# A hybrid decoder layer: turning the first two chunks by a matmul with a diagonal of the norm's powers

## The chip, the core and the metric

The kernel runs on one core of a Trainium2 chip. Such a core has a matrix engine (TensorE, PE in the profile), which multiplies a stationary 128x128 block by a moving one and writes to the accumulator memory PSUM; VectorE (DVE), ScalarE (ACT) and GpSimd (POOL) for element-wise work; and SyncE (SP), which here issues loads and stores. Each engine works through its own list of instructions in order, and waits on semaphores for the others. The metric is the device time of one execution in microseconds. The kernel before took 927.2 us, the median of three runs (926.85 to 927.48).

## The reference

One decoder layer in float32 on 512 tokens of 1024 features. Three stages follow each other, each with a norm ahead and behind it:

```python
def rms_norm(x, g):
    y = x * rsqrt(mean(x * x, axis=-1, keepdims=True) + EPS)
    return y * g

def swiglu_ffn(x, w_in, w_out):                    # w_in 1024 x 5632, w_out 2816 x 1024
    gate, up = split(x @ w_in, 2, axis=-1)
    return (silu(gate) * up) @ w_out

x = x + 0.5 * rms_norm(swiglu_ffn(rms_norm(x, norm_pre[0]), ffn1_w_in, ffn1_w_out), norm_post[0])
x = x + rms_norm(token_mixer(rms_norm(x, norm_pre[1]), ...), norm_post[1])
x = x + 0.5 * rms_norm(swiglu_ffn(rms_norm(x, norm_pre[2]), ffn2_w_in, ffn2_w_out), norm_post[2])
```

The change touches only the first `rms_norm` and the first products behind it. There, a token's row of x is multiplied by one number, its *power* r = (mean of squares + EPS) to the -1/2, and by the *weights* g, one per feature. The products need the result turned: features on the partitions, tokens along the free dimension.

## The kernel before

**Chunks, halves, parts.** The 512 tokens are four chunks of 128; chunk i lies in `xs[:, i, :]`, tokens on the partitions. The 1024 features are two halves of 512. Precision is kept by splitting each operand into a high part (a copy rounded to fp32r) and a low part (the rest); a product then is three matmuls, high by high, high by low and low by high. A high part is a copy, made on ACT; a low part is a subtraction on DVE. For a weight tile (128 x 4 x 256) `split` does both: `cast` has the copy (L244) and the subtraction (L245). For the turned x, `part` does them: L321 and L323, and later a plain copy for sums of halves (L325).

**The first feed-forward stage** multiplies with fewer products than the plain scheme would need, by sums and differences of quarters of weights and of x (the Strassen kind). The first column pair of the weights is done without that: four products named c1, c3, c2, c4 (in this order) for chunks 0 and 1, and e1 to e4 for chunks 2 and 3; p1 to p7 are those of the later column pairs. Each is a call of `prod` (L615), 24 matmuls of 256 columns (L628). c1 and c3 multiply the *first* half of the turned x with two weight tiles (`sq_84`, `sq_85`); c2 and c4 multiply the *second* half. c1 takes its parts in the order high by high, low weights, low x, the others in the order high by high, low x, low weights.

**The start** is written out by hand (`start`, inside a block in which the framework doesn't reorder), so the order of the code is the order on each engine. Ahead of it, `gain_pe` loads the row of 1024 weights and spreads it to all partitions by two matmuls with a column of ones (L123), which DVE copies from PSUM to `gpre` (L124). Then `norm(0)` and `norm(1)` run `pre`: ACT squares each half with a sum (L387); POOL makes the mean in two steps (L388) and raises it to -1/2 (L392); DVE multiplies each half by power and weights in one instruction (L403), into the tile `xn` for chunk 0 and into rows of the big buffer `hf` for chunk 1. PE turns a half by four transposes with the identity (L301, in `turn`). `spin` adds matmuls of the identity by itself (L130), whose result nobody reads; they fill PE's time at three places.

```python
self.spin(3)
step(q[0][0], q[0][1], q[0][0])   # turn chunk 0, both halves; high part of its first half
self.spin(2)
split = self.split()
step(q[1][0], q[1][1])            # turn chunk 1, both halves
next(split)                       # high part of the first weights, on ACT
step(q[1][0])                     # high part of chunk 1's first half
next(split)
step(q[0][0], q[1][0])            # low parts of both
```

After that `start` goes on: product c1, the next weights, high and low parts of the second halves, product c3, `norm(2)`, c2, `norm(3)`, and so on; chunks 2 and 3 are turned by transposes between the products (`sums`, L334 and L335). In the names of the order below, a trailing number is that of a buffer or of its use: `ps` are PSUM banks, `xn` and `hf` rows to be turned, `xq` the turned x with its parts, `sq` and `w` weights with their parts, `raw` weights as loaded, `col` single columns.

Of the kernel before, what the change touches and what calls it, by code (L numbers as in the profile page):

```python
# [11 lines left out]
ALU = mybir.AluOpType  # L12
# [12 lines left out]
EARLY = 2  # L25
HALF = T // 2
KH = ND // 2
FILL = (15, 12, 2, 2)
NH = 4
W = 512  # L30
# [41 lines left out]
class Layer:  # L72
# [37 lines left out]
    def gain_pe(self, tag, row):  # L110

        nc = self.nc
        g = self.cp.tile([P, D], F32, tag=tag, bufs=1, name=self.name(tag))
        r = self.hf[0:1, 14:16, :].rearrange("p a t -> p (a t)")
        nc.sync.dma_start(r, row)
        one = self.st("one", P)[:1]
        nc.gpsimd.memset(one, 1.0)
        self.spare = self.ps()
        self.spin(2)
        for h in range(2):  # L120
            ps = self.ps()
            v = slice(512 * h, 512 * h + 512)
            nc.tensor.matmul(ps, one, r[:, v], start=True, stop=True)  # L123
            nc.vector.tensor_copy(g[:, v], ps)  # L124
        return g

    def spin(self, n):
# [67 lines left out]
    def load(self, ld):  # L195
        self.nc.sync.dma_start(self.raw[ld.key], ld.src)

    def split(self):

        nc = self.nc  # L200
        it = self.items.popleft()
        raw = self.raw[it.key]
        _, a, b = raw.shape
        if it.dst:
            w = it.dst()
        else:
            if self.wt is None:
                self.wt = self.wp.tile([P, (2 * D + 128) * WBUF], F32R, name="w")

            n = self.free.popleft()  # L210
            o = PAD + (2 * D + 128) * n - 16 * (it.late if it.late is not None else b == 512)
            w = self.wt[:, o : o + 2 * D].rearrange("p (b k t) -> p b k t", b=2, k=a)
            if it.apart:
                w = tuple(self.wt[:, v : v + D].rearrange("p (k t) -> p k t", k=a) for v in (o, o + D + 16))
            self.slot[id(w)] = n, w
        hi, lo = self.both(w)
        self.ready.append((w, it.dst is not None))
        rows = it.rows
        if rows is None:
            yield from self.cast(hi, lo, raw, it.defer)  # L220
# [12 lines left out]
        if it.then:  # L233
            it.then(raw)
        self.load_due(self.done)
        self.done += 1
        yield

    def cast(self, hi, lo, src, defer=False):

        nc = self.nc
        late, self.pend = self.pend, ()
        steps = [
            lambda: nc.scalar.copy(hi, src),  # L244
            lambda: nc.vector.tensor_tensor(lo, src, hi.bitcast(F32), op=ALU.subtract),  # L245
        ]
# [46 lines left out]
        nc.gpsimd.tensor_tensor(r, m, self.nhalf[:, :n], op=ALU.pow)  # L293
        return r

    def turn(self, src, h):

        pt = self.ps()
        for c in range(4):
            k = 4 * h + c  # L300
            self.nc.tensor.transpose(pt[:, c * P : (c + 1) * P], src[:, k * P : (k + 1) * P], self.ident)  # L301
        return pt.rearrange("p (c t) -> p c t", c=4)

    def two(self, dst, i, src):
# [7 lines left out]
        for h in halves:  # L312
            self.two(self.xq[2 * (i // 2) + h], i, self.turn(src, h))

    def part(self, i, h, src):

        pv = self.turn(src, h)
# [3 lines left out]
        self.nc.scalar.copy(hi, pv)  # L321
        yield
        self.nc.vector.tensor_tensor(lo, pv, hi.bitcast(F32), op=ALU.subtract)  # L323
        yield
        self.nc.scalar.copy(self.xf[h][:, :, v], pv)  # L325
        yield
# [390 lines left out]
        self.hold = ()  # L717
        self.holes()

    def start(self, norm, xn):  # L720

        norm(0)
        norm(1)
        q = [[self.part(i, h, xn[i]) for h in range(2)] for i in range(2)]
        step = lambda *gs: [next(g) for g in gs]
        self.spin(3)
        step(q[0][0], q[0][1], q[0][0])
        self.spin(2)
# [987 lines left out]
def layer(tc, aps):  # L1716
    with ExitStack() as ctx:
# [26 lines left out]
        with ExitStack() as f1:  # L1744
            L.open_ffn(f1)
            with tc.manual_schedule():
# [13 lines left out]
                L.start(norm, xn)  # L1760
# [39 lines left out]
```

## Time and profile before

| what | value |
|---|---|
| median of three runs | 927.2 us |
| the profiled execution | 926.35 us |
| its span | 924.6 us |
| PE busy | 916.0 us, 7032 instructions |
| DVE, ACT, POOL busy | 765.2, 479.9, 285.2 us |
| first product (L628) starts | 11.63 us |
| granted clock, mean | 0.998 |

The span is what the profiler recorded from the first to the last instruction; the time of an execution has 1.75 us around it. In rows of instructions stand the start, the time that they were busy, engine, line, operation, what is written and read, sizes and a count, and in brackets the idle time of the engine ahead of them with what ended it. PEld is the loading of PE's stationary blocks, which runs beside its matmuls. A matmul's record lasts longer than the step to the next one, because matmuls overlap; steps are counted from start to start.

### The profile page before, as it was taken

To read this page: it belongs to the slowest core of one execution; us is meant where nothing else is said; L and a number is where in the kernel's file an instruction comes from. 1 tells how busy PE (TensorE), PEld (TensorE's weight loads), DVE (VectorE), ACT (ScalarE), POOL (GpSimd) and SP (SyncE) were. 2 spreads that over 40 slices of the span, in tenths; PEclk is the share of its full clock that TensorE was granted. 3 is DMA by queue.
4 is the path that set the end of the run, shared out by engine and by line. 5 is a ranking of instruction groups with operands and counts; after the bars stand their busy time and mean duration, and the time that the engine had idled before them with its cause. 6 is when DMAs were issued, how large, how long until landed. Compare 5 with 4: busy or idle time off the path is not lost.

```text
span 924.6 us, 16960 instructions
## 1 busy us (share of the span) xinstructions
PE 916.0 (99%) x7032; PEld 843.1 (91%) x7032; DVE 765.2 (83%) x899; ACT 479.9 (52%) x653; POOL 285.2 (31%) x225
## 2 busy tenths in 40 slices
PE   9999999999999999999999999999999999999997
PEld 7999999999888889888888888999999999988885
DVE  6898999999869786788766655888999999976874
ACT  7644445445544455987654254853444445544441
POOL 3535565562000026000020301445455665100001
PEclk9999999999999999999999999999999999999999
DMA  9243324332322413422423135213334332232302
GB/s 320 91 138 115 115 92 136 117 115 69 100 106 90 116 46 94 113 70 71 138 71 113 47 107 190 91 45 116 115 99 130 123 106 93 69 117 100 103 23 92
DMA packets 81991, 97.10 MB, mean 105 GB/s; under 512 B 4177, under 2 KB 61557, under 8 KB 81914
## 3 DMA queue, kind: packets, MB, share of 16 engines
q1 hardware_dynamic: 81306, 94.44, 32.1%
q8 instruction: 55, 0.90, 0.4%
q0 software_dynamic: 320, 1.06, 0.3%
q10 hardware_dynamic: 288, 0.52, 0.2%
q14 instruction: 22, 0.18, 0.1%
HBM read 93.90 MB, written 2.11 MB: 104 GB/s over the span
## 4 chain that ended last, share of the span: by engine, by line
PE 98%; issue 0%; ACT 0%; DMA 0%; DVE 0%; POOL 0%; DVEq 0%; POOLq 0%; ACTq 0%
PE ps L628 46%; PE ps L134 11%; PE ps L136 11%; PE ps L135 11%; PE ps L854 6%; PE ps L464 6%; PE ps L301 1%; PE ps L477 1%; PE ps L1302 1%; PE ps L1569 0%; PE ps L123 0%; PE ps L1537 0%; PE ps L1373 0%; PE ps L1341 0%; PE ps L1539 0%
## 5 line engine op out<-in xcount | busy, mean ns | idle before, releaser
L245 DVE TENSOR_TENSOR w<-raw,w 128x1024 fp32r<-128x1024 f32 x224 | 374.4, 1682 | 52.9 <-ACT w L244 52.7
L244 ACT CAST w<-raw 128x1024 fp32r<-128x1024 f32 x224 | 233.1, 1052 | 258.5 <-POOL raw L232 104.8
L232 POOL TENSOR_TENSOR raw<-raw,raw 128x1024 f32<-128x1024 f32 x80 | 221.0, 2764 | 174.2 <-DVE w L245 163.7
L628 PE MATMUL ps<-xq,w 128*128 128x256 f32 x2016 | 238.1, 277 | 0.0
L628 PEld LDWEIGHTS ps<-xq,w 128*128 128x128 f32 x2016 | 233.7, 188 | 0.2
L628 PE MATMUL ps<-sq,w 128*128 128x256 f32 x1440 | 169.8, 276 | 0.0
L628 PEld LDWEIGHTS ps<-sq,w 128*128 128x128 f32 x1440 | 166.2, 188 | 0.0
L134 PE MATMUL ps<-w,hs 128*128 128x512 f32 x240 | 93.6, 390 | 0.0
L135 PE MATMUL ps<-w,hs 128*128 128x512 f32 x240 | 93.5, 389 | 0.0
L136 PE MATMUL ps<-w,hs 128*128 128x512 f32 x240 | 93.4, 389 | 0.0
L134 PE MATMUL ps<-w,xq 128*128 128x512 f32 x208 | 83.2, 400 | 0.1
L135 PE MATMUL ps<-w,xq 128*128 128x512 f32 x208 | 81.0, 390 | 0.0
L136 PE MATMUL ps<-w,xq 128*128 128x512 f32 x208 | 80.9, 391 | 0.0
L388 POOL TENSOR_SCALAR col<-col 128x1 f32<-128x1 f32 x24 | 6.5, 273 | 200.2 <-ACT junk L387 200.1
L136 PEld LDWEIGHTS ps<-w,hs 128*128 128x128 f32 x240 | 45.1, 188 | 9.4
L134 PEld LDWEIGHTS ps<-w,hs 128*128 128x128 f32 x240 | 45.1, 188 | 8.8
L135 PEld LDWEIGHTS ps<-w,hs 128*128 128x128 f32 x240 | 45.1, 188 | 8.7
L464 PE MATMUL ps<-xq,w 128*128 128x512 f32 (+1 forms) x240 | 49.8, 368 | 0.0
L464 PEld LDWEIGHTS ps<-xq,w 128*128 128x128 f32 x240 | 41.3, 188 | 7.6 <-issue 0.2
L136 PEld LDWEIGHTS ps<-w,xq 128*128 128x128 f32 x208 | 39.0, 188 | 8.8 <-DVE xq L308 0.3
L134 PEld LDWEIGHTS ps<-w,xq 128*128 128x128 f32 x208 | 39.1, 188 | 8.6 <-ACT xq L307 0.7
L135 PEld LDWEIGHTS ps<-w,xq 128*128 128x128 f32 x208 | 39.1, 188 | 7.3
(259 smaller groups left out, 1108.8 us busy)
## 6 DMA issues: line engine op xcount, KB each, us to landing
raw<-in_ffn_w_in_dram SPq DMA_DIRECT2D x88, 512.0 KB, 4.5
raw<-in_ffn_w_out_dram SPq DMA_DIRECT2D x44, 512.0 KB, 3.6
raw<-in_w_mix_in_dram SPq DMA_DIRECT2D x28, 512.0 KB, 3.8
raw<-in_w_mix_out_dram SPq DMA_DIRECT2D x8, 512.0 KB, 3.6
out_dram<-xs SPq DMA_DIRECT2D x8, 256.0 KB, 2.1
xs<-in_x_dram SPq DMA_DIRECT2D x6, 256.0 KB, 6.2
gpost<-in_norm_post_dram SPq DMA_DIRECT2D x3, 512.0 KB
gpre<-in_norm_pre_dram SPq DMA_DIRECT2D x2, 512.0 KB, 4.1
```

The lines of the kernel that those rows point to most:

```text
L134: mm(ps, sh, mh, start=start, stop=False, **kw)
L135: mm(ps, sh, ml, start=False, stop=False, **kw)
L136: mm(ps, sl, mh, start=False, stop=stop, **kw)
L232: nc.gpsimd.tensor_tensor(o, o, c, op=ALU.add)
L244: lambda: nc.scalar.copy(hi, src),
L245: lambda: nc.vector.tensor_tensor(lo, src, hi.bitcast(F32), op=ALU.subtract),
L301: self.nc.tensor.transpose(pt[:, c * P : (c + 1) * P], src[:, k * P : (k + 1) * P], self.ident)
L464: mm(self.cols(ps, u0, u1), self.both(w)[a][:, k, :], self.xop(k, b, u0, u1), start=k + n + m == 0, stop=k == ND - 1 and n == 2, skip_grou ...
L477: self.nc.tensor.matmul(ps[:, :HALF], self.both(w)[a][:, k, :], self.xop(k, b, 0, HALF), start=m + k == 0, stop=m == 2 and k == ND - 1)
L628: self.nc.tensor.matmul(ps[:, c], wb[b][:, k, v], left[d][:, k, :], start=first and a + n + k == 0, stop=n == 2 and k == KH - 1, skip_grou ...
L854: self.nc.tensor.matmul(out, a[:, x, ka, tok(qa, t)], b[y][:, kb, col(qb)], start=p in sums and p not in begun, stop=stop and last[p, t] = ...
L1302: nc.tensor.matmul(sc[r, o : o + u.stop - u.start], k8[:, m, r], q8[:, m, u], start=True, stop=True, skip_group_check=True)
```

## The change

- `gain_pe` only does the two matmuls. The first half of the weights is copied from PSUM by DVE, in `start`, the second by ACT (L758 of the new file).
- For chunks 0 and 1, `start` does the norm itself. ACT squares all four halves; DVE makes the means (`mean`, L735); POOL still raises to -1/2 (L738). DVE multiplies rows by the weights alone (`gain`, L741), which waits for no power, and builds a 128x128 diagonal of the chunk's powers from the identity (`diag`, L745).
- `turn` has an argument `by`. With it, each of the four blocks is turned by an ordinary f32 matmul whose moving operand is the diagonal (L304), so that turning and multiplying by the powers are one step. Chunks 2 and 3, and all later uses, keep the transposes (L302).
- Only the first halves are turned ahead of c1. The row products of the second halves come behind the weights of c1 on DVE, and their turns behind c1 on PE.
- The high part of the first weights (`sq_84`) is made by DVE instead of ACT.
- Fillers are 2, 2 and 1 instead of 2, 3 and 2.

PE, from the fillers behind the weights' row to the third product, before: turns (L301), fillers (L130), products (L628).

```order
L130 MATMUL ps_101<-ident 128x128 x3
L301 MATMUL ps_160<-ident,xn_140 128x128 x4
L301 MATMUL ps_165<-ident,xn_140 128x128 x4
L130 MATMUL ps_101<-ident 128x128 x2
L301 MATMUL ps_173<-ident,hf_82 128x128 x4
L301 MATMUL ps_178<-ident,hf_82 128x128 x4
L628 MATMUL ps_190<-xq,sq_84 128x256 x24
L628 MATMUL ps_221<-xq,sq_85 128x256 x24
L628 MATMUL ps_190<-xq,w 128x256 x24
```

The same place on PE now (turns L304, fillers L129, products L631); the diagonal lies in `hf`, as do the rows of chunk 1.

```order
L129 MATMUL ps_101<-ident 128x128 x2
L304 MATMUL ps_158<-hf_82,xn_126 128x128 x4
L129 MATMUL ps_101<-ident 128x128
L304 MATMUL ps_166<-hf_82 128x128 x4
L631 MATMUL ps_178<-xq,sq_84 128x256 x24
L304 MATMUL ps_207<-hf_82,xn_126 128x128 x4
L304 MATMUL ps_212<-hf_82 128x128 x4
L631 MATMUL ps_221<-xq,sq_85 128x256 x24
L631 MATMUL ps_178<-xq,w 128x256 x24
```

Two of the four turns moved from ahead of c1 to between c1 and c3, and three fillers became two, two became one.

DVE, from its first instruction to the low part of c2's weights, as the difference of the two lists (`-` before, `+` now).

```order
-L124 COPY gpre_97<-ps_104 128x512
-L124 COPY gpre_97<-ps_107 128x512
-L403 TENSOR_SCALAR xn_140<-xs,col_138,gpre_97 128x512 x2
-L403 TENSOR_SCALAR hf_82<-xs,col_153,gpre_97 128x512 x2
+L1832 UNCONDITIONAL_BRANCH
+L735 TENSOR_SCALAR col_139<-col_127 128x1
+L751 COPY gpre_97<-ps_104 128x512
+L735 TENSOR_SCALAR col_142<-col_130,col_139 128x1
+L741 TENSOR_TENSOR xn_126<-xs,gpre_97 128x512
+L745 TENSOR_SCALAR hf_82<-ident,col_144 128x128
+L741 TENSOR_TENSOR hf_82<-xs,gpre_97 128x512
+L735 TENSOR_SCALAR col_149<-col_133 128x1
```

Ahead of the first diagonal DVE now copies half the weights and multiplies half a row; the second halves' row products are gone from here and stand behind the low parts of the first halves, as the next rows show.

```order
+L244 COPY sq_84<-raw_89 128x1024
 L245 TENSOR_TENSOR sq_84<-raw_89,sq_84 128x1024
-L323 TENSOR_TENSOR xq<-ps_160,xq 128x4x128
-L323 TENSOR_TENSOR xq<-ps_173,xq 128x4x128
+L326 TENSOR_TENSOR xq<-ps_158,xq 128x4x128
+L326 TENSOR_TENSOR xq<-ps_166,xq 128x4x128
+L741 TENSOR_TENSOR xn_126<-xs,gpre_97 128x512
+L741 TENSOR_TENSOR hf_82<-xs,gpre_97 128x512
 L245 TENSOR_TENSOR sq_85<-raw_91,sq_85 128x1024
```

The copy of the first weights is new on DVE; the two row products stand between the low parts for c1 and the low part of c3's weights.

The core of the diff:

```diff
+SPIN = (2, 2, 1)
...
-        self.spin(2)
-        for h in range(2):
-            ps = self.ps()
-            v = slice(512 * h, 512 * h + 512)
-            nc.tensor.matmul(ps, one, r[:, v], start=True, stop=True)
-            nc.vector.tensor_copy(g[:, v], ps)
+        self.spin(SPIN[0])
+        self.gained = [self.ps() for _ in range(2)]
+        for h, ps in enumerate(self.gained):
+            nc.tensor.matmul(ps, one, r[:, 512 * h : 512 * h + 512], start=True, stop=True)
...
+        copy = copy or nc.scalar.copy
...
-            lambda: nc.scalar.copy(hi, src),
+            lambda: copy(hi, src),
...
-    def turn(self, src, h):
+    def turn(self, src, h, by=None):
 
         pt = self.ps()
         for c in range(4):
-            k = 4 * h + c
-            self.nc.tensor.transpose(pt[:, c * P : (c + 1) * P], src[:, k * P : (k + 1) * P], self.ident)
+            o, x = pt[:, c * P : (c + 1) * P], src[:, (4 * h + c) * P : (4 * h + c + 1) * P]
+            if by is None:
+                self.nc.tensor.transpose(o, x, self.ident)
+            else:
+                self.nc.tensor.matmul(o, x, by, start=True, stop=True)
...
-    def start(self, norm, xn):
-
-        norm(0)
-        norm(1)
-        q = [[self.part(i, h, xn[i]) for h in range(2)] for i in range(2)]
-        step = lambda *gs: [next(g) for g in gs]
-        self.spin(3)
-        step(q[0][0], q[0][1], q[0][0])
-        self.spin(2)
-        split = self.split()
-        step(q[1][0], q[1][1])
-        next(split)
-        step(q[1][0])
-        next(split)
+    def start(self, norm, xn, g):
+
+        nc = self.nc
+        xg, ss, m, r, by = [self.xn_tile(i) for i in range(2)], {}, [EPS, EPS], {}, {}
+        v = lambda h: slice(512 * h, 512 * h + 512)
+
+        def square(i, h):
+            ss[i, h] = self.col()
+            nc.scalar.activation(self.junk(), self.xs[:, i, v(h)], AF.Square, accum_out=ss[i, h])
+
+        def mean(i, h):
+            before, m[i] = m[i], self.col()
+            nc.vector.tensor_scalar(m[i], ss[i, h], 1.0 / D, before, op0=ALU.mult, op1=ALU.add)
+            if h:
+                r[i] = self.col()
+                nc.gpsimd.tensor_tensor(r[i], m[i], self.nhalf[:, :1], op=ALU.pow)
+
+        def gain(i, h):
+            nc.vector.tensor_tensor(xg[i][:, v(h)], self.xs[:, i, v(h)], g[:, v(h)], op=ALU.mult)
+
+        def diag(i):
+            by[i] = self.hf[:, 8, i * P : (i + 1) * P]
+            nc.vector.tensor_scalar(by[i], self.ident, r[i], None, op0=ALU.mult)
+
+        for i in range(2):
+            for h in range(2):
+                square(i, h)
+        mean(0, 0)
+        nc.vector.tensor_copy(g[:, v(0)], self.gained[0])
+        mean(0, 1)
+        gain(0, 0)
+        diag(0)
+        gain(1, 0)
+        mean(1, 0)
+        mean(1, 1)
+        nc.scalar.copy(g[:, v(1)], self.gained[1])
+        step = lambda *gs: [next(p) for p in gs]
+        q = [[self.part(i, h, xg[i], self.hf[:, 8, i * P : (i + 1) * P]) for h in range(2)] for i in range(2)]
+        self.spin(SPIN[1])
+        step(q[0][0], q[0][0])
+        diag(1)
+        self.spin(SPIN[2])
+        step(q[1][0], q[1][0])
+        for _ in self.split(nc.vector.tensor_copy):
+            pass
         step(q[0][0], q[1][0])
...
         prod()
+        gain(0, 1)
+        gain(1, 1)
         self.full_split()
-        step(q[0][1], q[1][1], q[0][1], q[1][1])
+        step(q[0][1], q[1][1], q[0][1], q[1][1], q[0][1], q[1][1])
         prod()
```

More of the change, by code (lines that the diff above doesn't have):

```diff
@@ L196, in load, with split @@
         self.nc.sync.dma_start(self.raw[ld.key], ld.src)
-    def split(self):
+    def split(self, copy=None):
         nc = self.nc
@@ L219, in split @@
         if rows is None:
-            yield from self.cast(hi, lo, raw, it.defer)
+            yield from self.cast(hi, lo, raw, it.defer, copy)
         else:
@@ L237, in split, with cast @@
         yield
-    def cast(self, hi, lo, src, defer=False):
+    def cast(self, hi, lo, src, defer=False, copy=None):
         nc = self.nc
+        copy = copy or nc.scalar.copy
         late, self.pend = self.pend, ()
         steps = [
-            lambda: nc.scalar.copy(hi, src),
+            lambda: copy(hi, src),
             lambda: nc.vector.tensor_tensor(lo, src, hi.bitcast(F32), op=ALU.subtract),
@@ L313, in to_t, with part @@
             self.two(self.xq[2 * (i // 2) + h], i, self.turn(src, h))
-    def part(self, i, h, src):
-        pv = self.turn(src, h)
+    def part(self, i, h, src, by=None):
+        pv = self.turn(src, h, by)
         v = slice(i * P, (i + 1) * P)
@@ L1759, in layer @@
                     L.load(first.popleft())
-                L.start(norm, xn)
+                L.start(norm, xn, gp[0])
             L.small_params()
```

## The prediction

> **What bounds the kernel now.** I read the page's first part, then PE's waits, then busy time by stretch, then the chain of waits of the first 30 us, and last the engines' instructions one by one.
>
> ```profile
> span 924.6 us, 16960 instructions
> ...
> PE 916.0 (99%) x7032; PEld 843.1 (91%) x7032; DVE 765.2 (83%) x899; ACT 479.9 (52%) x653; POOL 285.2 (31%) x225
> ...
> PE 98%; issue 0%; ACT 0%; DMA 0%; DVE 0%; POOL 0%; DVEq 0%; POOLq 0%; ACTq 0%
> ```
>
> ```profile
> PE ps L130 <- POOL ident masks.py:199: 1.6, 1, 1.6
> PE ps L123 <- DMA hf<-in_norm_pre_dram: 0.3, 1, 0.3
> ```
>
> ```profile
> core 0: us, PE busy (x) PEld busy (x) DVE busy (x) ACT busy (x) POOL busy (x), PEclk, DMA share, GB/s
> ...
> 6.78:11.63 4.85, 4.71 (x27) 4.20 (x26) 4.05 (x6) 2.86 (x6) 2.06 (x4) 1.00 1.06 377
> 11.63:20.06 8.43, 8.43 (x73) 8.43 (x74) 7.63 (x10) 8.04 (x17) 3.37 (x5) 1.00 1.09 349
> ```
>
> PE is 98% of the chain, and its only waits that are listed lie in the first 3 us. From 11.63 us on, PE is busy for the whole of each stretch. So from the first product on, the time is the sum of PE's own work: whatever PE does in addition there is added to the end one for one, and whatever is saved ahead of it is a gain only if the first product starts earlier. The chain of waits shows what sets that start:
>
> ```profile
> 6.85 1.58 PE ps L130 x6
> 8.43 0.99 PE ps L301 x4
> 9.43 0.02 issue
> 9.45 0.59 ACT xq L321
> 10.04 0.94 ACT sq L244
> 10.98 0.01 issue
> 10.99 0.59 ACT xq L321
> 11.59 0.04 issue
> 11.63 8.58 PE ps L628 x72
> 20.22 0.88 PE ps L301 x8
> ```
>
> Fillers (L130), the first four transposes (L301), the high part of chunk 0 on ACT (L321), the first weights' high part (L244), the high part of chunk 1, then products: 72 matmuls in 8.58 us, 0.119 each. The c3 group, the second 24 of them, thus starts at 11.63 + 24 x 0.119 = 14.49. The last row prices a transpose at full clock: 0.88 / 8 = 0.11.
>
> PE's rows by time, and the durations of the filler's records:
>
> ```profile
> 6.78 1.65 PE L130 MATMUL ps<-ident 128*128 128x128 f32 x6
> 8.30 1.78 PE L301 MATMUL ps<-ident,xn 128*128 128x128 f32 x8
> 9.91 0.61 PE L130 MATMUL ps<-ident 128*128 128x128 f32 x4
> 10.36 1.13 PE L301 MATMUL ps<-ident,hf 128*128 128x128 f32 x8
> ...
> 20.06 1.03 PE L301 MATMUL ps<-ident,xn 128*128 128x128 f32 x8
> ```
>
> ```profile
> L130 PE MATMUL ps<-ident x14: 275/421/582, 1.6 to 10.2; 128*128 128x128 f32 x14
> ```
>
> An ordinary f32 matmul of 128 columns leaves two records (two fillers are four), a transpose one. Four filler records from 9.91 take (0.61 - 0.275) / 3 = 0.11 a step, as a transpose does; six from 6.78 take (1.65 - 0.42) / 5 = 0.25, with a longer first step, and I take 0.22 for later ones. So an ordinary turn costs twice a transposing one, and PE ran at half speed until about 9.7.
>
> **The change, part by part.** The other engines' rows, in order of time:
>
> ```profile
> 5.18 0.69 DVE L124 COPY gpre<-ps 128x512 f32<-128x512 f32 x1 [5.18 <-PE ps L123]
> ...
> 5.78 0.18 ACT L387 ACTIVATION_READ_ACCUMULATOR junk<-xs 128x1 f32 x1
> ...
> 6.49 0.56 POOL L392 TENSOR_TENSOR col<-col,nhalf 128x1 f32<-128x1 f32 x1
> ...
> 7.29 0.19 ACT L387 ACTIVATION_READ_ACCUMULATOR junk<-xs 128x1 f32 x1
> 7.50 1.41 DVE L403 SCALAR_TENSOR_TENSOR xn<-xs,col,gpre 128x512 f32<-128x512 f32 x2
> ...
> 8.46 0.87 POOL L392 TENSOR_TENSOR col<-col,nhalf 128x1 f32<-128x1 f32 x1
> ...
> 9.93 1.05 ACT L244 CAST sq<-raw 128x1024 fp32r<-128x1024 f32 x1
> ...
> 11.01 1.23 DVE L245 TENSOR_TENSOR sq<-raw,sq 128x1024 fp32r<-128x1024 f32 x1 [0.24 <-ACT sq L244]
> ...
> 12.16 1.28 DVE L323 TENSOR_TENSOR xq<-ps,xq 128x512 fp32r<-128x512 f32 x2
> ...
> 13.73 1.05 ACT L244 CAST w<-raw 128x1024 fp32r<-128x1024 f32 x1 [0.22 <-DMA raw<-in_ffn_w_in_dram]
> ...
> 15.49 0.19 POOL L388 TENSOR_SCALAR col<-col 128x1 f32<-128x1 f32 x1 [6.17 <-ACT junk L387]
> ...
> 17.05 0.63 ACT L387 ACTIVATE junk<-xs 128x512 f32<-128x512 f32 x1
> ...
> 17.70 1.41 DVE L403 SCALAR_TENSOR_TENSOR xn<-xs,col,gpre 128x512 f32<-128x512 f32 x2 [0.80 <-POOL col L392]
> ...
> 18.48 2.03 ACT L325 COPY hf<-ps 128x512 f32<-128x512 f32 x4
> 18.74 1.56 POOL L388 TENSOR_SCALAR col<-col,col 128x1 f32<-128x1 f32 x1 [0.24 <-ACT junk L387]
> ```
>
> *Norm of chunk 0.* One copy of the weights and a row op now stand ahead of the diagonal, and nothing there waits for the second half of the weights. The first copy ends at 5.87, the second sum at 5.96. No row shows a 128x1 op on DVE; POOL's power on one column (0.56) and zero bound it, and I take 0.1. The row op (no row has this form; between DVE's copy, 0.69, and half of L403's 1.41) ends near 6.85. POOL's power beside it takes 0.56 to 0.87, since the same op took 0.87 beside a DVE row op, and ends by 7.2. The 128x128 diagonal has no row either: between zero and a 512-wide copy's 0.69; I take 0.2, nearer to the small end because a quarter of the columns are read. It is ready at 7.4, at most 7.9.
>
> *Fillers and first turns.* Four filler records from 6.78 end at 7.78, so the fillers, not the norm, release the first turn. Its 8 records at half speed take 8 x 0.22 = 1.76, to 9.54; the two filler records, one at each speed, run to 9.9. The second diagonal follows the fourth sum (7.48), chunk 1's row op (to 8.2), two small means, a power (0.56 to 0.87) and 0.2: 9.2 to 9.6, hidden under the filler. The second turn at full speed takes 8 x 0.11 = 0.88, to 10.8, and its last record ends 0.16 later. ACT's high part takes 0.59. With three gaps of 0.03 between engines the first product starts at 11.6, against 11.63. Bounds: 11.0 (full speed from the start) to 12.0 (second diagonal late). I take 0.1 earlier, since the bound on the early side is farther.
>
> *High part of the first weights on DVE.* ACT loses 1.05, which no longer separates its two casts. DVE's copy has no row: half of L245's 1.23 to all of it. From 9.5 at the latest it ends by 10.7, under the second turn; L245 by 12.0, wanted after eight products (12.5); the two low parts of x (1.28) by 13.3, wanted after sixteen (13.5). Cost nothing; that cover is 0.2 at the upper bound.
>
> *Means to DVE, a weights copy to ACT.* POOL loses four 128x1 ops, DVE gains four. ACT copies the second half of the weights after its fourth square, 7.5 to 8.1, ahead of a cast that waits for PE until 9.7. Nothing. SP's order is unchanged; the weight load that waits for the first raw tile gets it at 12.0 instead of 12.24.
>
> *Second halves turned behind c1.* Before, these eight transposes lay ahead of 11.63, between waits. Now two turns, 16 records, stand between c1 and c3, and c3 uses neither of them: it multiplies the first half again. The row ops that feed them end by 14.7 at the latest, wanted at 14.4 (the first by 14.0) and 15.3. PE has no wait there that could absorb them, so 16 x 0.11 = 1.76 is added in full. Half of it, 0.88, would be added by transposes in this place.
>
> *What is late behind it.* ACT's casts of the second halves follow those turns, at 15.5 and 16.4, and all that is behind them in its queue moves along: the cast of c2's weights from 13.73 to 17.0. It ends at 18.0; c2 wants it at 16.2 + 24 x 0.119 = 19.1. Next come the two squares of chunk 2 (0.63 and a 0.19 read each), POOL's two steps (0.19 the shortest shown) and its power (0.56), then DVE's two row ops (1.41). From the start of that cast to the end of the row ops it was 17.70 + 1.41 - 13.73 = 5.38 before; the pieces alone are 1.05 + 1.64 + 0.38 + 0.56 + 1.41 = 5.04, and less where an op starts before the one ahead has quite ended. PE wants the rows at 20.06 + 1.7 = 21.8, and they come at 21.9 to 22.4. The wait is 0 to 0.6; I take 0.1, since the low part of those weights on DVE (1.23), which stretched POOL's second step before, now follows its cast at once and ends ahead of that step. The four copies (2.03) and the casts behind move alike; the first that PE wants from there, the high part of chunk 3, keeps some 0.8 of cover.
>
> *Sum:* -0.1 + 1.76 + 0.1 = +1.76. The profiled execution took 926.35 (its span and 1.75 around it) and would take 928.1; it is 0.85 below the median of the runs, 927.2, to which I add the same: 929.0, or 0.19% more.
>
> **A rule that speaks against the change.** The filler and transpose rows give a factor of two between an ordinary f32 matmul and a transpose. The Trainium skill, "TensorE: Matmul & The Clock Gate", section Terms, says that the transpose mode is four times faster for FP32. By that rule the sum would be +5.2 instead of +1.76; how, stands under the third rival.
>
> **The rivals.** A difference of 0.2% is 1.85 us, about what a measurement of this kernel can tell from none. The forecast lies just under that line.
>
> *Third chunk held by POOL (slower).* POOL's 128x1 step at 18.74 took 1.56 where its shortest kin take 0.2 to 0.3: it ended when DVE's row ops and L245, back to back, did. If one of chunk 2's two steps meets such a pair, the rows come 1.29 later and PE waits at their turn: 1.76 + 1.3 = 3.1, 930.3. It decides once the step starts inside a DVE pair, instead of the 0.2 us or so behind L245 that I reckon. For it: DVE has one more large op in its queue; against: L245 is then the last of them, and DVE waits for that power.
>
> *The clock opens earlier (same).* With full speed from 6.78 the first turn is done by 8.8 and the second waits for its diagonal: 9.3 + 0.88 + 0.16 + 0.65 = 11.0 to 11.2. That is 0.5 gained: +1.25, 928.4. For it: ordinary matmuls stand where transposes stood. Against: ten filler records (14 less the four from 9.91) before 8.3 did not do it, and c1 still starts with the second diagonal. The Trainium skill, the same title, Part 4, says that transpose mode does not count as PE activity for the clock in the same way; here the speed-up came while transposes ran, behind fillers, which neither proves nor refutes it.
>
> *Four for one (slower).* Turns at four times a transpose: 16 steps of 0.22 at half speed, of which 1.9 us fit ahead of 9.7, end the first at 10.5; the filler and 16 x 0.11 end the second at 12.5, c1 starts at 13.3 (+1.7), and 32 x 0.11 = 3.5 follow behind it: +5.2, 932.4. Against it the filler rows, the same kind of matmul.
>
> *Faster.* This needs c1 before 8.0, 1.76 + 1.85 ahead of today. Chunk 1's last sum is read at 7.48, and its power, turn and cast (0.56 + 0.88 + 0.59) alone lead past 9.5. Only a wait in front of c3 that covered the turns could do it, and the row of that stretch has none.
>
> **How the numbers follow.** Forecast mechanism 0.72: its own range is +1.4 to +2.2 (c1 from -0.4 to +0.2, the wait from 0 to 0.3), of which I put 0.42 under the 0.2% line and 0.30 over it. POOL's hold 0.12 (slower), earlier clock 0.08 (same), four for one 0.02 (slower), something that gains 0.04, other waits 0.02 (slower). Faster 0.04, same 0.50, slower 0.46. The range of 927.8 to 930.3 runs from a little past the earlier clock to POOL's hold, and leaves out both ends of the rest.
>
> **What would show it.** Right: c1 starts at 11.3 to 11.8, L304 behind it has 16 records in 1.76 us, c3 starts near 16.2, and from there PE runs without waits, all later rows 1.6 to 2 us late. Wrong: c1 before 11 or after 12; a PE wait at the turn of chunk 2 or on a cast; records of L304 that are fewer or longer; or later stretches shorter than before.

## The result, and the profile after

The changed kernel takes 930.2 us, the median of six runs (929.56 to 933.59); the kernel before, run beside it, 926.85 (926.21 to 927.48). The ratio is 1.004, with a 95% interval of 1.003 to 1.005: the change costs 3.35 us where 1.8 were forecast. The profiled execution took 930.13, 3.78 more than that of before.

The page of the changed kernel, its span and busy times:

```profile
span 928.4 us, 16985 instructions
...
PE 918.9 (99%) x7044; PEld 845.6 (91%) x7044; DVE 763.7 (82%) x905; ACT 480.1 (52%) x653; POOL 283.4 (31%) x221
```

PE is still busy for nearly the whole span, 2.9 us more than before. Its waits (total, times, longest) have changed:

```profile
PE ps L129 <- POOL gb L1154: 1.6, 1, 1.6
PE ps L631 <- ACT xq L324: 0.7, 1, 0.7
PE ps L631 <- ACT hf L658: 0.5, 1, 0.5
```

The first lies at the very start, as before. The second is the wait for the cast ahead of c1, where PE turned the second halves before. The third is new, and it is one wait on ACT, far behind the place that was changed. PE's rows show where (start, busy time, and in brackets the idle time ahead):

```profile
2.72 3.78 PE L123 MATMUL ps<-hf,one 1*128 1x512 f32 x4
...
7.67 2.08 PE L304 MATMUL ps<-hf,xn 128*128 128x128 f32 x8
...
9.97 1.73 PE L304 MATMUL ps<-hf 128*128 128x128 f32 x8
12.37 3.02 PE L631 MATMUL ps<-xq,sq 128*128 128x256 f32 x24 [0.68 <-ACT xq L324]
15.24 1.05 PE L304 MATMUL ps<-hf,xn 128*128 128x128 f32 x8
16.12 1.06 PE L304 MATMUL ps<-hf 128*128 128x128 f32 x8
16.94 3.05 PE L631 MATMUL ps<-xq,sq 128*128 128x256 f32 x24
19.82 2.88 PE L631 MATMUL ps<-xq,w 128*128 128x256 f32 x24
22.71 1.09 PE L302 MATMUL ps<-ident,xn 128*128 128x128 f32 x8
...
43.74 2.88 PE L631 MATMUL ps<-xq,sq 128*128 128x256 f32 x24
47.16 3.09 PE L631 MATMUL ps<-xq,w 128*128 128x256 f32 x24 [0.54 <-ACT hf L658]
50.19 0.25 PE L1137 MATMUL ps<-ident,rows 36*128 36x36 f32 x1
```

The same rows of the kernel before (c1 and c3 are one row there; c3 starts at 14.54, its 25th matmul):

```profile
11.63 5.86 PE L628 MATMUL ps<-xq,sq 128*128 128x256 f32 x48
17.33 2.88 PE L628 MATMUL ps<-xq,w 128*128 128x256 f32 x24
...
41.08 2.88 PE L628 MATMUL ps<-xq,sq 128*128 128x256 f32 x24
43.80 2.88 PE L628 MATMUL ps<-xq,w 128*128 128x256 f32 x24
46.61 0.25 PE L1101 MATMUL ps<-ident,rows 36*128 36x36 f32 x1
```

The last row of each fence is one small matmul with the same place in both programs; I call it the marker. Three pieces of time can be counted from starts of rows: c1 starts 0.74 later (12.37 against 11.63); from c1 to c3 it is 4.57 against 2.91, 1.66 more, the 16 turn records (from 15.24 to 16.94 they take 1.70); from c3 to the marker it is 33.25 against 32.07, 1.18 more. In sum 3.58 at the marker. The wait at p2(2) is listed with 0.54, but more of the last piece belongs to it: p2(2) starts 3.42 behind the product ahead of it (43.74 to 47.16) instead of 2.72, 0.70 more, and takes 3.03 to the marker instead of 2.81, 0.22 more. The turn of chunk 2 starts 2.89 behind c2 instead of 2.73, 0.16 more.

The chain of waits of the changed kernel, followed back from there, no longer runs through PE from c1 on, but through ACT and DVE:

```profile
22.45 1.93 ACT hf L328 x4
24.39 0.95 ACT w L244
...
26.81 1.28 ACT L653
...
31.14 1.89 DVE w L245
...
46.63 0.49 ACT hf L658
...
47.16 2.86 PE ps L631 x22
```

ACT works without a pause from 18.65 to 31.1; behind that it and DVE release each other in turn. Where this begins is seen in ACT's rows, first after (L324 are the casts of the second halves), then before (L321):

```profile
16.32 0.59 ACT L324 CAST xq<-ps 128x512 fp32r<-128x512 f32 x1 [3.06 <-PE ps L304]
17.22 0.59 ACT L324 CAST xq<-ps 128x512 fp32r<-128x512 f32 x1 [0.31 <-PE ps L304]
17.70 1.05 ACT L244 CAST w<-raw 128x1024 fp32r<-128x1024 f32 x1
...
35.07 0.59 ACT L338 CAST sq<-ps 128x512 fp32r<-128x512 f32 x1 [3.96 <-DVE ps L337]
...
46.49 0.62 ACT L658 COPY hf<-ps 128x512 f32<-128x512 f32 x1
```

```profile
12.43 1.07 ACT L321 CAST xq<-ps 128x512 fp32r<-128x512 f32 x2
...
42.85 0.61 ACT L655 COPY hf<-ps 128x512 f32<-128x512 f32 x1
```

The cast of c2's weights, `w`, starts at 17.70 instead of 13.73, 3.97 later, behind two casts that wait for PE while ACT idles for 3.06. The copy that p2(2) needs is 3.64 later 29 us on, while PE would have been only 2.7 late. ACT's idle time of 3.96 ahead of 35.07 gives nothing back: it waits there for DVE, which had begun behind ACT's late cast (31.14), and it idled 4.09 at the same place before. Before, that copy ended at 43.46, and p2(2) started at 43.80: a cover of 0.34.

### The profile page after: what moved, and what is told of

The parts are those of the page before. It is cut to its first block, busy times and chain, and to the rows that moved or that the text cites. A ratio compares the mean times of both kernels' runs of the same rounds, so it can differ in the third digit from the quotient of the medians.

```text
span 928.4 us, 16985 instructions
## 1 busy us (share of the span) xinstructions
PE 918.9 (99%) x7044; PEld 845.6 (91%) x7044; DVE 763.7 (82%) x905; ACT 480.1 (52%) x653; POOL 283.4 (31%) x221
## 3 DMA queue, kind: packets, MB, share of 16 engines
q0 software_dynamic: 320, 1.06, 0.4%
## 4 chain that ended last, share of the span: by engine, by line
PE 93%; ACT 2%; DVE 1%; issue 1%; POOL 0%; DVEq 0%; POOLq 0%; ACTq 0%
PE ps L631 43%; PE ps L133 11%; PE ps L135 11%; PE ps L134 11%; PE ps L890 6%; PE ps L467 6%; PE ps L480 1%; PE ps L302 1%; PE ps L1338 1%; PE ps L1605 0%; ACT w L244 0%; PE ps L1573 0%; DVE ps L337 0%; PE ps L1409 0%; ACT xq L338 0%
## 5 line engine op out<-in xcount | busy, mean ns | idle before, releaser
L631 PE MATMUL ps<-xq,w 128*128 128x256 f32 x2016 | 238.3, 277 | 0.5 <-ACT hf L658 0.5
L631 PEld LDWEIGHTS ps<-xq,w 128*128 128x128 f32 x2016 | 233.8, 188 | 0.9 <-ACT hf L658 0.7
L631 PE MATMUL ps<-sq,w 128*128 128x256 f32 x1440 | 169.8, 276 | 0.0
L631 PEld LDWEIGHTS ps<-sq,w 128*128 128x128 f32 x1440 | 166.2, 188 | 0.0
```

The source lines that it names most:

```text
L631: self.nc.tensor.matmul(ps[:, c], wb[b][:, k, v], left[d][:, k, :], start=first and a + n + k == 0, stop=n == 2 and k == KH - 1, skip_grou ...
```

## The experiments

Theory A, formed from these rows: the 16 records cost 1.7; the casts of the second halves hold up ACT's queue, which has no idle time of its own to give back, and its lateness reaches PE at chunk 2's turn and at p2(2) for 1.2; the rest is c1's start, which depends on when PE goes to full speed. The rivals: only PE's own work and speed count (B); VectorE and GpSimd set the new wait (C); the late c1 belongs to the change (D). The table has the outcome of all runs; the three columns of times are read from PE's rows of the one profiled execution, as above.

| kernel | median us (range) | c1 starts | c1 to c3 | c3 to marker |
|---|---|---|---|---|
| before | 926.85 (926.21 to 927.48) | 11.63 | 2.91 | 32.07 |
| after | 930.20 (929.56 to 933.59) | 12.37 | 4.57 | 33.25 |
| c2's weights first | 929.96 (929.12 to 932.28) | 12.46 | 4.58 | 32.16 |
| second halves ahead of c1 | 928.63 (928.49 to 929.17) | 13.75 | 2.85 | 32.07 |
| second halves by transposes | 929.41 (928.28 to 930.72) | 13.34 | 3.73 | 33.22 |
| before, second halves moved | 928.38 (927.93 to 931.85) | 12.77 | 6.06 | 33.26 |
| after, again | 930.29 (929.56 to 930.82) | 11.54 | 4.57 | 33.23 |
| after, full columns | 929.97 (929.90 to 930.19) | 12.45 | 4.59 | 33.16 |
| before, full columns | 927.04 (926.83 to 927.74) | 12.10 | 2.88 | 32.07 |
| transposes and c2's weights first | 928.51 (927.72 to 931.64) | 13.35 | 3.65 | 32.26 |
| before, full columns, row late | 926.89 (926.26 to 928.52) | 11.80 | 2.92 | 32.07 |
| the same, norm reordered | 927.78 (926.71 to 928.43) | 12.24 | 2.87 | 32.07 |

The kernel before had medians of 926.79, 927.12 and 926.83 beside the three groups of experiments (four, four and two runs).

**c2's weights first.**

```diff
         self.full_split()
+        self.full_split()
         step(q[0][1], q[1][1], q[0][1], q[1][1], q[0][1], q[1][1])
         prod()
-        self.full_split()
         norm(2)
```

> The changed kernel, with one thing moved: the high and low parts of c2's weights are made ahead of the parts of the second halves of x, so ACT makes the high part in its idle time near 13.8 us instead of at 17.70, and everything behind it in ACT's queue starts about 1 us earlier. PE has the same instructions in the same order. Theory A (a queue on ACT, late because of the casts of the second halves, runs on to the fourth of the later products and makes PE wait there): c1 and c3 start as before this edit (12.4 and 16.9 if PE gets to full speed at the same time), the 0.54 us wait of p2(2) for the copy of p1(2)'s result goes, chunk 2's turn waits less; 0.5 to 0.9 us less than the changed kernel, some 929.4. Theory B (all of the loss is PE's own work and its speed at the start): the end does not move, 930.2. Theory C (VectorE and GpSimd, not ACT, set that wait): the wait stays.

```profile
14.44 1.05 ACT L244 CAST w<-raw 128x1024 fp32r<-128x1024 f32 x1 [1.08 <-DMA raw<-in_ffn_w_in_dram]
16.42 0.58 ACT L324 CAST xq<-ps 128x512 fp32r<-128x512 f32 x1 [0.94 <-PE ps L304]
...
45.60 0.62 ACT L658 COPY hf<-ps 128x512 f32<-128x512 f32 x1
```

```profile
17.04 3.05 PE L631 MATMUL ps<-xq,sq 128*128 128x256 f32 x24
...
46.39 2.88 PE L631 MATMUL ps<-xq,w 128*128 128x256 f32 x24
49.20 0.25 PE L1137 MATMUL ps<-ident,rows 36*128 36x36 f32 x1
```

ACT's rows, then PE's. The cast of c2's weights now stands in the idle time, the copy for p2(2) is 0.89 earlier, and the wait is gone. From c3 to the marker it is 32.16, 1.09 less than after: theory A, and a little more than expected. The profiled execution took 929.12, 1.01 less than that of the changed kernel. The median fell by only 0.24; its five runs spread over 3.2 us, and the ratio to before, 1.0038 (1.0025 to 1.0051), doesn't separate it from the changed kernel. So the wait is shown by the trace, its price by the trace and by the later run that has this edit too, not by this median. Theory B is out. This run alone doesn't settle C, since the subtraction of c2's weights moves along on VectorE (15.52 instead of 18.79); against C stand the rows of the changed kernel, in which ACT has no pause ahead of 31.1, while VectorE waits for ACT at 29.22 (0.88), 30.20 (0.29) and 31.14 (0.26).

**Second halves ahead of c1.**

```diff
         for _ in self.split(nc.vector.tensor_copy):
             pass
+        gain(0, 1)
+        gain(1, 1)
         step(q[0][0], q[1][0])
+        step(q[0][1], q[1][1])
...
         prod()
-        gain(0, 1)
-        gain(1, 1)
         self.full_split()
-        step(q[0][1], q[1][1], q[0][1], q[1][1], q[0][1], q[1][1])
+        step(q[0][1], q[1][1], q[0][1], q[1][1])
```

> The changed kernel, with the turns of the second halves (still by the diagonal) ahead of c1, where PE waits for the cast of chunk 1 anyway. Theory A: c1 starts at about 13.2 to 13.8, c3 24 steps later at 16.1 to 16.6 (16.94 in the changed kernel), the casts of the second halves on ACT come 2 us earlier and the wait at p2(2) goes: 0.8 to 1.5 us less than the changed kernel, 928.7 to 929.4. Theory B (PE's work alone): only the 0.3 to 0.8 of c3, 929.4 to 929.9. If the place of the turns did not matter at all: 930.2.

```profile
11.94 1.16 PE L304 MATMUL ps<-hf,xn 128*128 128x128 f32 x8 [0.61 <-DVE xn L741]
...
13.75 5.81 PE L631 MATMUL ps<-xq,sq 128*128 128x256 f32 x48
```

c1 starts 1.38 later than in the changed kernel and everything behind it is as in the kernel before: 928.63, 1.57 less than the changed kernel, ratio 1.0022 (1.0013 to 1.0031). Moving the turns behind c1 thus bought 1.4 us ahead of c1 and paid 1.66 + 1.18 = 2.84 behind it.

**Second halves by transposes.** VectorE multiplies these rows by power and weights at once, as before.

```diff
+        def both(i):
+            nc.vector.scalar_tensor_tensor(xg[i][:, v(1)], self.xs[:, i, v(1)], r[i], g[:, v(1)], op0=ALU.mult, op1=ALU.mult)
...
-        q = [[self.part(i, h, xg[i], self.hf[:, 8, i * P : (i + 1) * P]) for h in range(2)] for i in range(2)]
+        q = [[self.part(i, h, xg[i], None if h else self.hf[:, 8, i * P : (i + 1) * P]) for h in range(2)] for i in range(2)]
...
-        gain(0, 1)
-        gain(1, 1)
+        both(0)
+        both(1)
```

> The changed kernel, with the second halves of chunks 0 and 1 turned in the same place behind c1, but by transposes: rows multiplied by power and weights in one step on VectorE, 8 records on PE instead of 16. If an ordinary turn costs two records of 0.11 where a transpose costs one: c3 is 0.88 earlier, and the casts on ACT as well, so the wait at p2(2) stays about as it was: 0.9 us less, 929.3. If the price of the turns is not what makes c3 late (they lie in a wait for something else): no change, 930.2. If an ordinary turn cost four transposes: more than 0.88, c3 2.6 earlier.

```profile
13.34 3.11 PE L631 MATMUL ps<-xq,sq 128*128 128x256 f32 x24 [0.68 <-ACT xq L324]
16.28 0.60 PE L302 MATMUL ps<-ident,xn 128*128 128x128 f32 x4
...
17.07 3.04 PE L631 MATMUL ps<-xq,sq 128*128 128x256 f32 x24
...
47.36 3.00 PE L631 MATMUL ps<-xq,w 128*128 128x256 f32 x24 [0.59 <-ACT hf L658]
```

From c1 to c3 it is 0.84 less (the 8 records take 0.79 from start to start, the 16 took 1.70): an ordinary turn costs two transposes, not four. (The Trainium skill, "TensorE: Matmul & The Clock Gate", Terms, has transposes four times faster for FP32; here the measured two decides.) The wait stays (0.59), as theory A has it, since the casts of the second halves are early by as much as PE is. 929.41, 0.8 less than the changed kernel, ratio 1.0027 (1.0016 to 1.0039).

**The kernel before, second halves moved.**

```diff
-        step(q[0][0], q[0][1], q[0][0])
+        step(q[0][0], q[0][0])
...
-        step(q[1][0], q[1][1])
+        step(q[1][0])
...
-        step(q[0][1], q[1][1], q[0][1], q[1][1])
+        step(q[0][1], q[1][1], q[0][1], q[1][1], q[0][1], q[1][1])
```

> The kernel before, with one thing done alone: the transposes of the second halves and their parts stand behind c1, as in the changed kernel; no diagonal, the same fillers, the first weights' high part still on ACT. Theory A: c1 at 11.2 to 11.6; 8 records of 0.11 between c1 and c3 (+0.88), and the casts of the second halves, which end near 12.9 + 0.6 before, end near 16.3, so the cast of c2's weights goes from 13.73 to 16.3 and ACT's queue arrives 2 us later at the later products: waits of PE at the turn of chunk 2 and at p2(2) that sum to 0.5 to 1.0; in all +1.4 to +1.9 on 926.85, 928.3 to 928.8. Theory B (PE's work alone): +0.5 to +0.9, 927.4 to 927.7. If the move costs nothing and the diagonal is all: 926.9.

```profile
10.98 1.11 PE L301 MATMUL ps<-ident,hf 128*128 128x128 f32 x4 [1.05 <-DVE hf L403]
12.77 5.43 PE L628 MATMUL ps<-xq,sq 128*128 128x256 f32 x24 [0.67 <-ACT xq L321]
...
18.83 3.04 PE L628 MATMUL ps<-xq,sq 128*128 128x256 f32 x24
...
49.15 3.01 PE L628 MATMUL ps<-xq,w 128*128 128x256 f32 x24 [0.57 <-ACT hf L655]
```

The median, 928.38, ratio 1.0020 (1.0011 to 1.0030), is 1.6 above the kernel before, as theory A has it and not B; the wait at p2(2) is there without any diagonal, and c3 to the marker is 33.26, the same 1.2 more. The place of the casts makes the wait, not the way in which the rows are turned. c1's own start was missed (12.77 for 11.2 to 11.6): in the profiled execution chunk 1 of x came late (its first square at 7.59, 6.00 in the kernel before), and c1 ran at half speed to its end (5.43 for 24 matmuls, against 3.0), behind two waits of PE of 1.05 and 0.67. That execution took 931.85, 3.5 above the median.

**The changed kernel again**, unaltered.

> The changed kernel once more, unaltered, to see how much of the start of c1 (12.37 us in its profile, 11.63 in the kernel before) belongs to the change and how much to one execution. Theory A: what lies behind c1 is fixed (c1 to the row behind p2(2): 37.8 us again, with the 0.5 us wait of p2(2)), while c1 itself starts anywhere from 11.3 to 13.3, with the time at which PE goes to full speed and at which x lands; the time of the whole follows c1 one for one. Theory D (the late c1 is part of the change): c1 at 12.3 to 12.5 again. Median 930.2 by both.

```profile
9.80 1.06 PE L304 MATMUL ps<-hf 128*128 128x128 f32 x8
11.54 3.04 PE L631 MATMUL ps<-xq,sq 128*128 128x256 f32 x24 [0.68 <-ACT xq L324]
...
46.31 3.09 PE L631 MATMUL ps<-xq,w 128*128 128x256 f32 x24 [0.57 <-ACT hf L658]
...
49.52 3.09 PE L631 MATMUL ps<-sq,w 128*128 128x256 f32 x24
52.45 2.99 PE L631 MATMUL ps<-xq,w 128*128 128x256 f32 x24
```

c1 starts at 11.54: its second turn ran at full speed (1.06 for eight records, 1.73 in the first profile). Theory D falls for c1's start in a single execution, and what lies behind c1 is the same to 0.02. That this execution is no faster (930.29) has its cause behind the marker: from 49.5 to 76 us the products of 24 matmuls came 2.83 apart instead of 2.72, which gave back 1.0 us. So single executions differ by a microsecond at both ends, and the distances between rows are a sharper measure of this change than the medians.

**Full columns.** The row of weights lies as 128 x 8, VectorE spreads it over 128 x 1024 with the identity, and the matmul that spreads it to all partitions has 128 rows instead of one; five fillers stand ahead of it instead of two. In the changed kernel and, in the same way, in the kernel before:

```diff
-SPIN = (2, 2, 1)
+SPIN = (5, 2, 1)
...
-        r = self.hf[0:1, 14:16, :].rearrange("p a t -> p (a t)")
-        nc.sync.dma_start(r, row)
-        one = self.st("one", P)[:1]
+        r = self.hf[:, 14:16, :].rearrange("p a t -> p (a t)")
+        w = self.hf[:, 13, :8]
+        nc.sync.dma_start(w, row.rearrange("o (p j) -> (o p) j", j=8))
+        one = self.st("one", P)
         nc.gpsimd.memset(one, 1.0)
+        for h in range(2):
+            at = slice(64 * h, 64 * h + 64)
+            nc.vector.tensor_tensor(
+                r[:, 512 * h : 512 * h + 512].rearrange("p (k j) -> p k j", j=8),
+                self.ident[:, at].unsqueeze(2).to_broadcast([P, 64, 8]),
+                w.unsqueeze(1).to_broadcast([P, 64, 8]),
+                op=ALU.mult,
+            )
```

> The changed kernel, but the norm's weights are spread to the partitions by matmuls with a full column of 128 ones (the row lies as 128 x 8, and VectorE spreads it over a 128 x 1024 block with the identity) instead of matmuls with one row, and five fillers stand ahead of them instead of two, so that PE has full-size work from 1.6 us on. In the five profiles so far PE got to full speed at the end of some 3.4 us in which it ran full-size work nearly without a pause, and never right behind the one-row matmuls (2.7 to 6.5 us). If those one-row matmuls don't count for the speed: full speed by 8.4 us at the latest, the first turns take about 1 us instead of 2.08, c1 starts at 11.1 to 11.6, 0.8 to 1.1 us less than the changed kernel: 929.1 to 929.4, with less spread. If the speed comes whatever PE does: c1 at 12.4, 930.2 to 930.6.

> The kernel before, with the same spread of the weights by full columns and five fillers. If one-row matmuls don't count for PE's speed: full speed by 8.4, c1 at 11.2 to 11.6 in every execution, 0 to 0.6 us less than the kernel before, 926.2 to 926.8, with less spread; the copies of the weights on VectorE are up to 0.5 later, which can take that back. Else: 926.8 to 927.3.

PE's rows of the changed kernel with full columns (lines are 9 higher), then the first square on ACT there:

```profile
4.14 2.57 PE L132 MATMUL ps<-hf,one 128*128 128x512 f32 x4
...
8.67 1.16 PE L313 MATMUL ps<-hf,xn 128*128 128x128 f32 x8 [1.51 <-DVE hf L754]
```

```profile
5.56 0.63 ACT L740 ACTIVATE junk<-xs 128x512 f32<-128x512 f32 x1 [2.34 <-DMA xs<-in_x_dram]
```

Full speed came inside the spreading matmuls (2.57 for four records; with one row they took 3.78), and the first turn takes 1.16 instead of 2.08. Yet c1 starts at 12.45, because x landed late: the first square starts at 5.56, in the first profiles at 4.5. The time from there to c1 is 6.89 (before, full columns: 6.95), against 7.82 in the changed kernel, 7.12 in its second profile and 7.14 in the kernel before. With full speed early in both, the medians differ by 929.97 - 927.04 = 2.93, of which 2.80 lies between c1 and the marker: 0.13 is left for all else. The gain that was expected didn't come: 929.97 is 0.3 below the changed kernel beside it (930.29), where 0.8 to 1.1 were forecast; 927.04 is 0.1 below the kernel before, where 0 to 0.6 were. The late landing explains c1 in this one profile, but not the medians. Against before the ratios are 1.0032 (1.0020 to 1.0044) and 0.9998 (0.9989 to 1.0006).

**Transposes and c2's weights first.** The edits of the first and the third experiment together.

> The changed kernel with two of its costs taken out at once: the second halves are turned by transposes behind c1, and c2's weights are made ahead of their parts. Theory A: c1 to c3 3.7 to 3.75 us (4.57 in the changed kernel), no wait at p2(2), c1 to the row behind p2(2) 37.8 - 0.88 - 0.95 = 36.0; 1.8 us less than the changed kernel, 928.4. What is left over the kernel before is then 8 records on PE (0.9) and c1's start. If the two are not independent (the wait returns once PE is earlier): 929.0 to 929.3.

Both costs go, each by its own amount: c1 to c3 3.65, c3 to the marker 32.26, together 35.91 (36.0 expected). 928.51, 1.8 below the changed kernel beside it, ratio 1.0017 (1.0008 to 1.0026). What is left between c1 and the marker is 0.93: 0.74 from c1 to c3, where the eight transposes stand, and 0.19 behind.

**An attempt to beat both.** The kernel before with full columns, the row of weights loaded behind chunk 0 of x:

```diff
-                gp[0] = L.gain_pe("gpre", pre[0:1, :])
                 for i in range(NT):
+                    if i == 1:
+                        gp[0] = L.gain_pe("gpre", pre[0:1, :])
```

> An attempt to beat both kernels: the kernel before with the weights spread by full columns, as in the run above, but their row is loaded behind chunk 0 of x instead of ahead of it (in the two runs with full columns the first square started at 5.15 and 5.56 us, 4.42 to 4.56 in most others), and seven fillers bridge the time. If the load of 128 short rows held x up: first square at 4.5, full speed by 8.4, c1 6.95 later (the distance in both runs with full columns), at 11.4 to 11.5, and c1 to the row behind p2(2) 34.9 as in the kernel before: 926.3 to 926.7, 0.2 to 0.6 less than the kernel before. If x's landing is chance and not that load: c1 at 11.4 to 12.1, 926.5 to 927.1.

x came early, the first square at 4.28, but now the weights are late: VectorE starts to spread them at 4.74, copies them from PSUM at 6.66 and 7.52, and the first row of x follows at 8.13. c1 at 11.80, 7.52 behind the first square where 6.95 was expected; 926.89, ratio 1.0008 (0.9999 to 1.0017). The eleven times lie in two groups, six from 926.26 to 926.89 and five from 928.35 to 928.52, and the median is the last of the lower group; the profiled execution, 926.26, is of that group, and why there are two was not found. In a second version ACT copies the second half of the weights and VectorE makes chunk 1's means (`power(1, nc.vector)`) behind the first row:

```diff
-            nc.vector.tensor_copy(g[:, v], ps)
+            if h:
+                self.gained = ps
+            else:
+                nc.vector.tensor_copy(g[:, v], ps)
...
+        nc.scalar.copy(g[:, 512:], self.gained)
+        power(0, nc.gpsimd)
+        row(0, 0)
+        power(1, nc.vector)
+        row(0, 1)
+        row(1, 0)
+        row(1, 1)
```

> The kernel above with the two parts of the change that lie on the path of the norm: ACT, not VectorE, copies the second half of the weights, so that the first row of x doesn't wait for that copy, and VectorE makes chunk 1's means right behind that row instead of GpSimd, which waits for VectorE's row operations there. Chunk 1's power is ready 0.2 to 0.4 earlier: c1 6.5 to 6.8 after the first square, 11.0 to 11.3; c1 to the row behind p2(2) 34.9; 926.0 to 926.5, 0.4 to 0.9 less than the kernel before. If the power only moves beside another row operation and takes longer for it (0.86 instead of 0.56): as the kernel above.

```profile
9.06 1.00 POOL L749 TENSOR_TENSOR col<-col,nhalf 128x1 f32<-128x1 f32 x1 [2.26 <-DVE col L746]
```

Chunk 1's power starts at 9.06 instead of 8.01, behind VectorE's means, which stand behind the first row, and beside a row operation of VectorE it takes 1.00 instead of the 0.56 of the first version. c1 starts at 12.24, in an execution of 927.00. The median is 927.78, ratio 1.0010 (1.0001 to 1.0019), and here too the times lie in two groups, five from 926.71 to 927.00 and six from 927.78 to 928.43. Both miss; no kernel run here is measurably faster than the kernel before.

## Why the prediction was wrong

It forecast +1.76, and +3.35 came. Step by step:

- *Norm, fillers, first turns:* the pieces were near what was taken. The first diagonal was there at 7.33 + 0.29 = 7.62 (forecast 7.4, at most 7.9), the second at 9.28 + 0.28 = 9.56 (9.2 to 9.6). The mean steps on VectorE took 0.15 and 0.21 (0.1), the diagonal 0.28 to 0.29 (0.2).
- *c1 at 11.6, bounds 11.0 to 12.0:* right for an execution in which PE speeds up as in the profile of before (11.54), wrong as a bound. "PE ran at half speed until about 9.7" was read from one execution and used as a property of the kernel. In the first profile of the changed kernel the second turn still ran mostly at half speed, and c1 came at 12.37. Ordinary turns have twice the records at that speed.
- *High part of the first weights on VectorE, cost nothing:* right; it took 0.69, from 9.48, and hid under the filler and the second turn.
- *Second halves behind c1, 16 x 0.11 = 1.76:* right. The distance from c1 to c3 was 1.66 to 1.68 more in all four profiles with these turns there, and 0.84 and 0.92 less than that in the two profiles with transposes.
- *What is late behind it, 0.1:* this step failed. At chunk 2's turn the wait was indeed small (about 0.16). But the text then followed ACT's queue only as far as "the first that PE wants from there, the high part of chunk 3", found 0.8 of cover, and stopped. There PE didn't wait. ACT however works back to back from 18.65 to 31.1, and its idle time behind that is a wait for VectorE, which is late by ACT's cast; so the 3.97 that the cast of c2's weights lost was handed on almost whole, 3.64, to the copy that p2(2) needs, where the cover had been 0.34 and PE only 2.7 late. The term measured 1.18; it was 1.09 to 1.19 in five profiles of four kernels that cast those weights last, and 0.1 to 0.2 in two that cast them first. The premise under it failed with it: from c1 on the time was no longer the sum of PE's own work.
- *The rivals:* that of the third chunk gave 930.3, near the result, but by another mechanism: chunk 2's turn lost only 0.16, not 1.3. Four for one is out by the third experiment. An earlier speed-up didn't come by itself; where fillers and full columns brought it, the median was 0.3 lower, which the spread of the two (929.56 to 930.82 and 929.90 to 930.19) doesn't separate.

So 1.66 + 1.18 = 2.84 of the 3.35 is shown, in rows that repeat from run to run. The other 0.5 (0.3 by the medians of the second measurement, 930.29 and 927.12) most likely lies ahead of c1. With full speed early it is 0.1, which fits later speed-ups that cost the double turns more; its cause was not shown, and the medians of the kernel before alone differ by 0.33 between two groups (926.79, 927.12).

## What to carry to other kernels

When work is moved behind another step, follow every queue that it holds up, not only to the next thing that someone wants, but until it idles for something that the same lateness hasn't reached. An engine at half load can be without a pause for 12 us just there, and an idle stretch behind that, here 3.96, absorbs nothing if the engine it waits for is late as well. Before moving a cast that must wait for PE, look at what stands behind it on its engine and can go first; here one moved line was worth 1.0 to 1.1 us in the rows behind it, in two pairs of kernels. And where a start-up depends on when an engine gets to full speed, count distances between rows behind that point, and take more than one execution for what lies ahead of it.

## What the hardware showed that was not expected

- **When PE speeds up.** Full speed is read from the step between matmuls of 128 columns, 0.21 us before and 0.11 after. In seven of the eight profiles with one-row matmuls it came between 9.7 and about 13 us, in one at 18; in all four with full columns it was there by 6.5, inside the spreading matmuls or ahead of them. That the one-row matmuls, 3.8 us of busy PE, did not count fits this, but was not shown: the four kernels also have five or seven fillers instead of two, and in one of them (row late, seven fillers) PE was at full speed at the first spreading matmul, 5.49. More fillers alone were not tried. The Trainium skill, "TensorE: Matmul & The Clock Gate", Part 1, says that PE gets its full clock behind a busy window of some 3.4 us, and that the windows run freely, not from the kernel's start. The spread from 9.7 to about 13 in kernels with nearly the same start agrees with free-running windows; what counts as busy for them the runs here don't show.
- **A late speed-up behind short waits.** In the one execution in which PE waited 1.05 and 0.67 us ahead of c1 behind its first turn, c1 ran at half speed to its end at 18 (5.43 instead of 3.0). That the waits put the speed-up off is possible, but was not tried apart: in the kernel with transposes and c2's weights first PE waited 1.30 ahead of its first turn and was at full speed by 12.
- **Casts.** A 128x1024 cast from f32 to fp32r took 0.69 on VectorE and 1.05 on ACT; the subtraction that follows it took 1.22.
- **Landing of x.** The first square started between 4.25 and 5.84 us, late in two kernels that hadn't changed the loads as well (5.34, 5.84). Whether the load of 128 short rows adds to that stayed open: 5.15 and 5.56 with it ahead of x, 4.25 and 4.28 with it behind chunk 0.
